# Eight weight units at other byte offsets, MoBA's score scale from a root of its own, and the first conv tap on ScalarE

## The chip, the cores and the metric

The kernel runs on one core of one Trainium2 chip. The metric is the device time of one execution, in microseconds, as the median of several executions. The engines are named as in the profile: PE is TensorE's matmul, PEld its weight load, DVE is VectorE, ACT is ScalarE, POOL is GpSimd, SP issues the DMAs.

## The reference

Two layers of a decoder trunk on x (256 tokens x 1024), all in float32. Each layer is a mixer and a feed-forward part (FFN):

```python
for l in range(DEPTH):                                   # 2
    sh1, sc1, g1, sh2, sc2, g2 = split(silu(c) @ w_mod[l] + b_mod[l], 6)
    h = rms_norm(x, mix_norm_g[l]) * (1 + sc1) + sh1
    x = x + g1 * token_mixer(h, ...)
    h = rms_norm(x, ffn_norm_g[l]) * (1 + sc2) + sh2
    x = x + g2 * channel_mixer(h, ...)

def token_mixer(h, ...):
    q_lat, kv_lat, k_rope, qkv_b, conv_in, gates = split(h @ w_in)
    o_a = MLA attention from q_lat, kv_lat, k_rope       # 8 heads
    q_b, k_b = rope(rms_norm(q, g)), rope(rms_norm(k, g))   # MoBA, 8 heads of 64
    o_b = softmax(causal(q_b @ k_b.T * 64 ** -0.5)) @ v  # one block of 256 tokens
    u = glu_a * sigmoid(glu_g)                           # 512 channels
    u = sum(w[t] * shifted(u, t) for t in range(31)) + b # causal depthwise conv
    o_c = silu(layer_norm(u)) @ w_conv_pw2 + b_conv_pw2
    return (sig(g0) * o_a @ w_mla_o + sig(g1) * o_b @ w_moba_o + sig(g2) * o_c) @ w_out

def channel_mixer(h, ...):
    a, b = split(causal_dwconv3(h @ w_up) + bias)        # 2 x 2816
    return (silu(a) * b) @ w_down
```

## The kernel before

**Weight units.** Nearly all of the matmul work goes through units. A unit is 128 x 1024 floats of weights (512 KB; some have 672 or 768 columns). SP loads it into a `raw` tile, `split` (L203) makes two fp32r tiles of it, `whi` on ACT (L210, a rounded copy) and `wlo` on DVE (L212, raw minus whi), and PE multiplies in three passes: high by high (L287), high by low of the activations (L288), low by high (L290). A unit of 1024 columns is eight 128 x 128 stationary tiles, so 24 matmuls of 256 columns. `take` (L252) hands out units in the order of `all_units` (L238) and keeps three ahead.

**Where a unit lies.** Each whi or wlo tile begins at a multiple of 512 bytes in a partition and has 128 spare columns; the unit stands in it from column `LEAD` = 16, which is 64 bytes, so every stationary tile begins at 64 bytes modulo 512. The activations that stream past (`hh`, `hl`, `oah`, `mhl` and so on) begin at 0 modulo 512.

**Order.** Each layer runs its mixer by a list of named steps, `STEPS` (L70): QKV are the MoBA projections, MS and MP the sums and the preparation for MLA, BS (`moba_rstd`, L935) and BP (`moba_prep`) the same for MoBA, MA and BA the attentions, C and G the gates, O the output projections of both attentions, V the conv taps, LN, LS, LB its layer norm, R and M the modulation of later stages, OC and PR the ends. Then come norm_stats and the FFN, in which `FFN` (L138) sets up and down units in turn: up 0, up 1, up 2, down 0, up 3 and so on, two units for each of the 22 ups, one for each down. The tile framework then schedules the instructions engine by engine, by priority in the order of the code and by its own estimate of when operands are ready; each engine runs its list strictly in order.

**MoBA's roots.** `rstd_of` (L493, L494) makes (sum * scale + eps) on DVE and raises it to -0.5 on POOL. `moba_rstd` squares q and k on ACT, sums 16 groups of 64 on DVE (L939), takes one root of 16 columns on POOL, and then DVE multiplies the 8 columns of q by 64 ** -0.5 (L942) to get `scb`, the scale of the scores. That L942 waits for POOL, and DVE's later work stands behind it.

**Conv taps.** `conv` (L1049) adds up 31 taps for each of 4 channel groups, all on DVE: tap 0 is a TENSOR_SCALAR that also adds the bias (L1054), the other 30 are L1057.

Of the kernel before, what the change touches and what calls it, by code (L numbers as in the profile page):

```python
# [10 lines left out]
F32R = mybir.dt.float32r  # L11
# [3 lines left out]
ALU = mybir.AluOpType  # L15
AX = mybir.AxisListType

P = 128
# [35 lines left out]

LINE = 512
LEAD = 16
TAILP = 2
FLEAD = 1
ROWS = [(0, 0), (0, 1), (1, 0), (1, 1)] + RPARTS
# [9 lines left out]

STEPS = [(  # L70
# [77 lines left out]
def trunk_kernel(ctx, tc, xT, crow, ccol, pos, invf, modb_d, cols_d, grow_d, wmh, wmr, wm, win1, wqkv,  # L148
# [11 lines left out]
    def nm(s):  # L160
        uid[0] += 1
        return f"{s}_{uid[0]}"
# [23 lines left out]
    def small(n, tag="sm", bufs=12):  # L186
        return wk.tile([P, n], F32, tag=tag, name=nm(tag), bufs=bufs)
# [12 lines left out]
    turn = [0]  # L200
    hold = [None]

    def split(raw):  # L203
        n = raw.shape[1]
        turn[0] += 1
        th, nh = hi_tags[turn[0] % len(hi_tags)]
        tl, nl = lo_tags[turn[0] % len(lo_tags)]
        hi, lo = (wk.tile([P, 1024 + 128], F32R, tag=t, name=nm(m), bufs=b, align_bytes=LINE)[:, LEAD:LEAD + n]
                  for t, m, b in ((th, "whi", nh), (tl, "wlo", nl)))
        ac.activation(hi, raw, AF.Copy)  # L210
        with tc.issue_after(hold[0]) if hold[0] else ExitStack():
            ve.tensor_tensor(lo, raw, hi.bitcast(F32), op=ALU.subtract)  # L212
        return hi, lo

    def chop(src, n, c, size=1024):

        m = max(1, size // c)
        return [(src[:, k0 * c:min(n, k0 + m) * c], range(k0, min(n, k0 + m))) for k0 in range(0, n, m)]

    def token_units(l, t):  # L220

        if t[0] == "KL":
            return [(win1[l, t[1], :, 0:672], [0])]
        if t[0] == "QKV":
            return [chop(wqkv[l, t[1], t[2] // 2], 4, 512)[t[2] % 2]]
        if t[0] in ("UQ", "UK"):
            return chop(wuq[l], 3, 768) if t[0] == "UQ" else chop(wukv[l], 2, 1024)
        if t[0] in ("C", "G"):
            return [chop((wgc if t[0] == "C" else wgab)[l, t[1]], KD, S)[t[2]]]
        if t[0] == "O":  # L230
            return chop(woab[l, t[1]], 1, 1024)
        if t[0] == "OC" and t[1] % 2 == 0:
            return chop(woc[l, t[1] // 2], 1, 1024)
        if t[0] == "PR" and t[1] % 2 == 0:
            return chop(wout[l, t[1] // 2], 2, 1024)
        return []

    def all_units():  # L238
        for l in range(L):
            for k in range(KD):  # L240
                if l == 0:
                    yield win1[l, k, :, 0:672], [0]
                yield win1[l, k, :, 672:1696], [0]
            for t in CFG["order"][l]:
                yield from token_units(l, t)
            for up, j in FFN:
                yield from chop(wup[l, j], KD, S) if up else chop(wdn[l, j], 1, 1024)

    ahead = [AHEAD0]
    coming, ready = list(all_units())[::-1], []  # L250
# [1 line left out]
    def take(n=1):  # L252

        while coming and len(ready) < n + ahead[0]:
            src, ks = coming.pop()
            ready.append((split(wload(src)), src.shape[1] // len(ks), ks))
        res = []
        for _ in range(n):
            (hi, lo), c, ks = ready.pop(0)
            res.append([(k, (hi[:, i * c:(i + 1) * c], lo[:, i * c:(i + 1) * c])) for i, k in enumerate(ks)])  # L260
        return res
# [226 lines left out]

    rst, rests = [None], []

    def rstd_of(ssum, n, scale):
        r = small(n, "rs", 8)
        rst[0] = ve.tensor_scalar(r, ssum, scale, EPS, op0=ALU.mult, op1=ALU.add)  # L493
        gp.tensor_tensor(r, r, mhalf[:, :n], op=ALU.pow)  # L494
        return r

# [198 lines left out]
    def layer(l):  # L695
# [239 lines left out]
        def moba_rstd(b):  # L935
            sq = mq()
            ac.activation(sq, qks[b], AF.Square)
            ss = small(16, "ss", 2)
            ve.tensor_reduce(ss, sq.rearrange("p (g d) -> p g d", d=64), axis=AX.X, op=ALU.add)  # L939
            rr = rstd_of(ss, 16, 1.0 / 64.0)  # L940
            sc = small(8, "scb", 4)
            ve.tensor_scalar(sc, rr[:, 0:8], 64 ** -0.5, None, op0=ALU.mult)  # L942
            scb.append(sc)
            rrb.append(rr)

        def moba_prep(b):
            if b == 0:
                pair = wk.tile([P, 2, 4, S], F32, tag="qkT", name=nm("qkTb"), bufs=2, align_bytes=LINE)
                qTb.append(pair[:, 0])
                kTb.append(pair[:, 1])  # L950
            rr = rrb[b]
            ra = qks[b]
            rb = mq()
            for t, i in ((rb, 1), (ra, 0)):
                for qk in range(2):
                    ve.tensor_tensor(t[:, qk * 512:(qk + 1) * 512].rearrange("p (h d) -> p h d", h=H),
                                     qks[b][:, qk * 512:(qk + 1) * 512].rearrange("p (h d) -> p h d", h=H),
                                     tb[:, i, b, qk, :].unsqueeze(1).to_broadcast([P, H, 64]), op=ALU.mult)
            av = ra.rearrange("p (g d) -> p g d", d=64)
            bv = rb.rearrange("p (g d) -> p g d", d=64)  # L960
            rope(av[..., 0:32], av[..., 32:64], av, bv, 32)
            kview = ra[:, 512:1024].rearrange("p (h d) -> p h d", h=H)
            ve.tensor_tensor(kview, kview, rr[:, 8:16].unsqueeze(2).to_broadcast([P, H, 64]), op=ALU.mult)
            for i, dst in ((0, qTb[0]), (1, kTb[0])):
                pt = psa()
                for c in range(4):
                    te.transpose(pt[:, c * P:(c + 1) * P], ra[:, i * 512 + c * P:i * 512 + (c + 1) * P], ident)
                ac.activation(dst[:, :, b * P:(b + 1) * P], pt.rearrange("p (c t) -> p c t", c=4), AF.Copy)
# [79 lines left out]
        def conv(j, t0, t1):  # L1048
            if not cacc:  # L1049
                cacc.append(wk.tile([P, 4, S], F32, tag="lh2", name=nm("cacc"), bufs=1))  # L1050
            aj = cacc[0][:, j, :]
            for t in range(t0, t1):
                if t == 0:
                    ve.tensor_scalar(aj, upad[:, j, 0:S], cw[:, j * 31:j * 31 + 1], cv(l, "cdw_b")[:, j:j + 1],  # L1054
                                     op0=ALU.mult, op1=ALU.add)
                else:
                    ve.scalar_tensor_tensor(aj, upad[:, j, t:t + S], cw[:, j * 31 + t:j * 31 + t + 1], aj,  # L1057
                                            op0=ALU.mult, op1=ALU.add)
# [301 lines left out]
```

## Time and profile before

| what | value |
|---|---|
| runs of the kernel | 928.8, 935.16, 941.89 us; median 935.16 |
| the profiled execution's own time | 937.53 us |
| its span in the profile | 935.3 us |
| PE busy | 905.6 us (97%) |
| DVE busy | 791.7 us (85%) |
| ACT busy | 554.7 us (59%) |
| POOL busy | 43.3 us (5%) |
| DMA read | 199.33 MB, 214 GB/s over the span |

Matmuls overlap each other in the pipeline, so PE can be called busy throughout a stretch and still deliver its matmuls at different spacings. For a stretch in which PE never idles, read the distance between the starts of equal instructions.

### The profile page before, as it was taken

The page shows a single profiled execution, that of the slowest core. Times are in us where ns is not written, and L with a number is a line of the kernel's source. Part 1 is how long each engine was busy: PE and PEld are TensorE (multiplying, and loading weights), DVE is VectorE, ACT ScalarE, POOL GpSimd, SP SyncE. Part 2 cuts the span into 40 slices and gives each one's busy share as a digit, 9 for nine tenths or more (in the row PEclk, how much of TensorE's full clock was granted, in tenths as well). Part 3 has the DMA queues.
Part 4 walks back from the last instruction along what each step waited for, and adds up shares of the span by engine and source line. Part 5 has one row for each costly group of instructions (what it writes and reads, how often), then busy time and mean ns, then how long its engine had stood idle before and what let it go on. Part 6 is the DMA issues. An engine that isn't in the chain of part 4 may idle for free.

```text
span 935.3 us, 18669 instructions
## 1 busy us (share of the span) xinstructions
PE 905.6 (97%) x7327; PEld 852.5 (91%) x7327; DVE 791.7 (85%) x1530; ACT 554.7 (59%) x980; POOL 43.3 (5%) x32
## 2 busy tenths in 40 slices
PE   6999989998999999999999999999999999999998
PEld 5988878988997999999979987889999799999998
DVE  6989899999987999997774999999787788777774
ACT  4677588644655655565543675895475565555551
POOL 0011500000000000000000042000000000000000
PEclk8999999999999999999999999999999999999999
DMA  8955524698868888876544565548657666655541
GB/s 308 384 194 199 181 93 165 195 320 299 301 232 287 283 266 295 298 229 193 184 151 129 184 232 182 195 129 278 223 181 264 208 226 207 189 187 189 183 134 46
DMA packets 57975, 201.59 MB, mean 216 GB/s; under 512 B 6944, under 2 KB 8480, under 8 KB 57888
## 3 DMA queue, kind: packets, MB, share of 16 engines
q1 hardware_dynamic: 57888, 200.41, 64.4%
q8 instruction: 57, 0.93, 0.4%
q14 instruction: 30, 0.25, 0.1%
HBM read 199.33 MB, written 1.05 MB: 214 GB/s over the span
## 4 chain that ended last, share of the span: by engine, by line
PE 80%; DVE 9%; DMA 5%; ACT 2%; POOL 2%; issue 2%; SPq 0%; POOLq 0%; DVEq 0%; ACTq 0%
PE psb L287 16%; PE psb L288 16%; PE psb L290 15%; PE psa L290 8%; PE psa L287 8%; PE psa L288 7%; DVE wlo L212 2%; DMA raw<-in_wmr 2%; PE psa L385 2%; POOL rs L494 2%; DVE cacc L1057 1%; PE psa L664 1%; PE psa L281 1%; PE psa L652 1%; PE psa L282 1%
## 5 line engine op out<-in xcount | busy, mean ns | idle before, releaser
L210 ACT ACTIVATE whi<-raw 128x1024 fp32r<-128x1024 f32 (+2 forms) x286 | 295.7, 1041 | 225.3 <-PE psb L288 108.4
L212 DVE TENSOR_TENSOR wlo<-raw,whi 128x1024 fp32r<-128x1024 f32 (+2 forms) x286 | 340.7, 1196 | 81.3 <-ACT whi L210 70.3
L287 PE MATMUL psb<-hh,whi 128*128 128x256 f32 x1088 | 266.3, 284 | 1.3 <-ACT thc L778 1.3
L288 PE MATMUL psb<-hl,whi 128*128 128x256 f32 x1088 | 263.1, 281 | 0.0
L287 PEld LDWEIGHTS psb<-hh,whi 128*128 128x128 f32 x1088 | 205.8, 190 | 8.7 <-issue 4.5
L288 PEld LDWEIGHTS psb<-hl,whi 128*128 128x128 f32 x1088 | 205.2, 189 | 1.4 <-DVE hl L561 1.1
L290 PE MATMUL psb<-hh,wlo 128*128 128x256 f32 x1088 | 151.2, 281 | 0.0
L290 PEld LDWEIGHTS psb<-hh,wlo 128*128 128x128 f32 x1088 | 137.4, 189 | 0.8 <-issue 0.8
L1057 DVE SCALAR_TENSOR_TENSOR cacc<-upad,cw,cacc 128x256 f32<-128x256 f32 x240 | 104.8, 480 | 0.1
L287 PE MATMUL psa<-mhl,whi 128*128 128x256 f32 x400 | 96.1, 281 | 0.0
L288 PE MATMUL psa<-mhl,whi 128*128 128x256 f32 x400 | 96.0, 281 | 0.0
L1236 DVE SCALAR_TENSOR_TENSOR e<-psb,fw,e 128x255 f32<-128x255 f32 (+1 forms) x176 | 83.9, 478 | 13.0 <-ACT e L1234 11.9
L287 PEld LDWEIGHTS psa<-mhl,whi 128*128 128x128 f32 x400 | 75.4, 189 | 0.0
L288 PEld LDWEIGHTS psa<-mhl,whi 128*128 128x128 f32 x400 | 75.4, 189 | 0.0
L494 POOL TENSOR_TENSOR rs<-rs,mhalf 128x16 f32<-128x16 f32 (+3 forms) x22 | 41.8, 1907 | 693.8 <-DVE rs L493 693.0
L1234 ACT ACTIVATE e<-psb,fb,fw 128x256 f32<-128x256 f32 x88 | 48.6, 552 | 28.3 <-DVE e L1236 14.2
L290 PE MATMUL psa<-mhl,wlo 128*128 128x256 f32 x400 | 55.0, 280 | 0.0
L368 DVE SCALAR_TENSOR_TENSOR raw<-raw,crow 128x1024 f32<-128x1024 f32 x40 | 48.9, 1222 | 4.6 <-DMA raw<-in_wmr 4.5
L290 PEld LDWEIGHTS psa<-mhl,wlo 128*128 128x128 f32 x400 | 50.5, 189 | 0.0
L287 PE MATMUL psb<-whi,hh 128*128 128x416 f32 (+1 forms) x96 | 31.6, 353 | 3.9 <-ACT hh L807 3.9
L1244 ACT ACTIVATE mhl<-e 128x256 fp32r<-128x256 f32 x44 | 18.3, 416 | 22.6 <-DVE e L1242 21.7
L288 PE MATMUL psb<-whi,hl 128*128 128x416 f32 (+1 forms) x96 | 30.7, 351 | 0.2 <-DVE hl L808 0.2
(272 smaller groups left out, 1475.3 us busy)
## 6 DMA issues: line engine op xcount, KB each, us to landing
raw<-in_wup SPq DMA_DIRECT2D x88, 512.0 KB, 4.6
raw<-in_wmr SPq DMA_DIRECT2D x52, 512.0 KB, 5.1
raw<-in_wdn SPq DMA_DIRECT2D x44, 512.0 KB, 4.3
raw<-in_wm SPq DMA_DIRECT2D x40, 512.0 KB, 4.3
raw<-in_wgab SPq DMA_DIRECT2D x32, 512.0 KB, 5.2
raw<-in_wqkv SPq DMA_DIRECT2D x24, 512.0 KB, 5.0
raw<-in_win SPq DMA_DIRECT2D x16, 512.0 KB, 4.3
raw<-in_wgc SPq DMA_DIRECT2D x16, 512.0 KB, 4.1
```

Source lines behind the costliest of these rows:

```text
L210: ac.activation(hi, raw, AF.Copy)
L212: ve.tensor_tensor(lo, raw, hi.bitcast(F32), op=ALU.subtract)
L287: te.matmul(o, p1[0], p1[1], start=start, stop=False)
L288: te.matmul(o, p2[0], p2[1], start=False, stop=False)
L290: te.matmul(o, p3[0], p3[1], start=False, stop=stop)
L368: ve.scalar_tensor_tensor(raw, raw, scale, row, op0=ALU.mult, op1=ALU.mult, accum_out=acc)
L385: te.matmul(acc[32 * c:32 * c + 32, 0:S], cact[:, k:k + 1].to_broadcast([P, 32]), raw[:, c * S:(c + 1) * S], start=(k == 0), stop=(k == KD ...
L494: gp.tensor_tensor(r, r, mhalf[:, :n], op=ALU.pow)
L1057: ve.scalar_tensor_tensor(aj, upad[:, j, t:t + S], cw[:, j * 31 + t:j * 31 + t + 1], aj, op0=ALU.mult, op1=ALU.add)
L1234: ac.activation(t, src, AF.Identity, scale=fw[:, 2, c:c + 1], bias=fb[:, c:c + 1])
L1236: ve.scalar_tensor_tensor(t[:, d:S], src[:, 0:S - d], fw[:, 2 - d, c:c + 1], t[:, d:S], op0=ALU.mult, op1=ALU.add)
L1244: ac.activation(mh, th, AF.Copy)
```

## The change

It has four parts. (1) Eight units get another offset, in four pairs that follow each other on PE: the first of a pair at 0, the second at 40 columns (160 bytes). The pairs are O6 and the first half of G7 in layer 0, the first half of G6 and O4 in layer 1, and the two halves of the FFN's up 2 in both layers. (2) `moba_rstd` takes two roots of 8 columns on POOL, first that of k, then that of q with the factor 64 folded into scale and eps, so that L942 goes. (3) In layer 0, BS0 and BS1 stand right behind MP0 and MP1. (4) Tap 0 of the conv is an activation on ACT.

```diff
+LEADS = {(0, "O", 6): 0, (0, "G", 7, 0): 40, (1, "G", 6, 0): 0, (1, "O", 4): 40}
+PAIRS = (2,)
...
-    "QKV13 QKV21 MP0 MP1 m0 QKV22 v0 MA00 MA01 MA10 MA02 BS0 MA03 MA04 C00 MA11 BS1 BP0 BP1 QKV23 C01 MA12 "
+    "QKV13 QKV21 MP0 BS0 MP1 BS1 m0 QKV22 v0 MA00 MA01 MA10 MA02 MA03 MA04 C00 MA11 BP0 BP1 QKV23 C01 MA12 "
...
-    def split(raw):
+    def split(raw, lead):
...
-        hi, lo = (wk.tile([P, 1024 + 128], F32R, tag=t, name=nm(m), bufs=b, align_bytes=LINE)[:, LEAD:LEAD + n]
+        hi, lo = (wk.tile([P, 1024 + 128], F32R, tag=t, name=nm(m), bufs=b, align_bytes=LINE)[:, lead:lead + n]
...
             for t in CFG["order"][l]:
-                yield from token_units(l, t)
+                yield from ((*u, LEADS.get((l, *t), LEAD)) for u in token_units(l, t))
             for up, j in FFN:
-                yield from chop(wup[l, j], KD, S) if up else chop(wdn[l, j], 1, 1024)
+                for i, u in enumerate(chop(wup[l, j], KD, S) if up else chop(wdn[l, j], 1, 1024)):
+                    yield *u, (0, 40)[i] if up and j in PAIRS else LEAD
...
-    def rstd_of(ssum, n, scale):
-        r = small(n, "rs", 8)
-        rst[0] = ve.tensor_scalar(r, ssum, scale, EPS, op0=ALU.mult, op1=ALU.add)
+    def rstd_of(ssum, n, scale, eps=EPS):
+        r = small(n, "rs", 12)
+        rst[0] = ve.tensor_scalar(r, ssum, scale, eps, op0=ALU.mult, op1=ALU.add)
...
-            rr = rstd_of(ss, 16, 1.0 / 64.0)
-            sc = small(8, "scb", 4)
-            ve.tensor_scalar(sc, rr[:, 0:8], 64 ** -0.5, None, op0=ALU.mult)
-            scb.append(sc)
-            rrb.append(rr)
+            rrb.append(rstd_of(ss[:, 8:16], 8, 1.0 / 64.0))
+
+            scb.append(rstd_of(ss[:, 0:8], 8, 1.0, 64.0 * EPS))
...
                 if t == 0:
-                    ve.tensor_scalar(aj, upad[:, j, 0:S], cw[:, j * 31:j * 31 + 1], cv(l, "cdw_b")[:, j:j + 1],
-                                     op0=ALU.mult, op1=ALU.add)
+                    ac.activation(aj, upad[:, j, 0:S], AF.Identity, scale=cw[:, j * 31:j * 31 + 1],
+                                  bias=cv(l, "cdw_b")[:, j:j + 1])
```

The pairs move nothing in any engine's list; the other parts do. The changed kernel's lines from 203 on stand two to four lower, so that L958 there is L956 here.

On DVE in layer 0, where MoBA's sums meet the first MLA attention (mq are MoBA's q and k, tb its rotary table, mx the row maxima and nb the biases of the MLA scores, cacc the conv's sum). Before:

```order
L493 TENSOR_SCALAR rs_1457<-ss_1455 128x16
L956 TENSOR_TENSOR mq_1463<-mq_923,tb_753 128x512
L1057 SCALAR_TENSOR_TENSOR cacc_1258<-upad_773,cw_762,cacc_1258 128x256
L612 TENSOR_REDUCE mx_1277<-psa_1264 128x2
L612 TENSOR_REDUCE mx_1277<-psa_1265 128x2
L942 TENSOR_SCALAR scb_1460<-rs_1457 128x8
L956 TENSOR_TENSOR mq_1463<-mq_923,tb_753 128x512
L615 TENSOR_SCALAR nb_1281<-mx_1277 128x8
```

And in the changed kernel, in the same place:

```order
L958 TENSOR_TENSOR mq_1465<-mq_923,tb_753 128x512
L1059 SCALAR_TENSOR_TENSOR cacc_1278<-upad_773,cw_762,cacc_1278 128x256
L613 TENSOR_REDUCE mx_1297<-psa_1283 128x4
L616 TENSOR_REDUCE mx_1297<-psa_1284 128x2
L616 TENSOR_REDUCE mx_1297<-psa_1285 128x2
L1059 SCALAR_TENSOR_TENSOR cacc_1278<-upad_773,cw_762,cacc_1278 128x256
L619 TENSOR_SCALAR nb_1301<-mx_1297 128x8
```

The sums of both row blocks now stand ahead of the maxima, and between the maxima and nb there is no instruction that reads a root from POOL.

On ACT in layer 0, behind the latents (klt are the KV latents, whi the units of the query and key-value projections). Before:

```order
L862 ACTIVATE klt_772<-psb_864,col_133 128x256
L210 ACTIVATE whi_889<-raw_887 128x768
L210 ACTIVATE whi_907<-raw_905 128x768
L210 ACTIVATE whi_929<-raw_927 128x1024
L896 ACTIVATE mq_923<-psa_810 128x512
```

And in the changed kernel:

```order
L866 ACTIVATE klt_772<-psb_864,col_133 128x256
L213 ACTIVATE whi_889<-raw_887 128x768
L1056 ACTIVATE cacc_1278<-upad_773,col_133,cw_762 128x256 x3
L213 ACTIVATE whi_907<-raw_905 128x768
L1056 ACTIVATE cacc_1278<-upad_773,col_133,cw_762 128x256
L213 ACTIVATE whi_929<-raw_927 128x1024
L900 ACTIVATE mq_923<-psa_810 128x512
```

The four taps stand between whi copies that are wanted by PE.

## Rows read from the trace of the kernel before

**Rows 1.** The page: busy time by engine, and the chain that ended last.

```profile
PE 905.6 (97%) x7327; PEld 852.5 (91%) x7327; DVE 791.7 (85%) x1530; ACT 554.7 (59%) x980; POOL 43.3 (5%) x32
...
PE 80%; DVE 9%; DMA 5%; ACT 2%; POOL 2%; issue 2%; SPq 0%; POOLq 0%; DVEq 0%; ACTq 0%
```

**Rows 2.** Timeline of PE, layer 1, conv input units: start, us, what, count.

```profile
490.38 1.07 PE L290 MATMUL psa<-hh,wlo 128*128 128x256 f32 x8
...
506.70 1.07 PE L290 MATMUL psa<-hh,wlo 128*128 128x256 f32 x8
```

**Rows 3.** Chain in order of time, FFN of layer 0: start, us, what.

```profile
309.05 0.94 PE psa L290 x8
...
467.35 0.94 PE psa L290 x8
```

**Rows 4.** Timeline of PE, FFN of layer 0, second half of up 2.

```profile
304.80 0.28 PE L288 MATMUL psb<-hl,whi 128*128 128x256 f32 x1
305.55 0.44 PE L393 MATMUL psa<-ident,e 128*128 128x128 f32 x2 [0.47 <-ACT e L390]
305.75 0.36 PE L287 MATMUL psb<-hh,whi 128*128 128x256 f32 x1
305.95 0.28 PE L288 MATMUL psb<-hl,whi 128*128 128x256 f32 x1
306.06 1.10 PE L290 MATMUL psb<-hh,wlo 128*128 128x256 f32 x8
```

**Rows 5.** Timeline of PE, layer 1, around the conv norm's broadcast (L523).

```profile
675.78 0.50 PE L290 MATMUL psb<-hh,wlo 128*128 128x256 f32 x3
676.12 0.60 PE L523 MATMUL psb<-ident,rs 128*128 128x128 f32 x4
678.45 1.11 PE L290 MATMUL psb<-hh,wlo 128*128 128x256 f32 x8
```

**Rows 6.** Stretches: PE, PEld, DVE, ACT, POOL busy (count), PEclk, DMA share, GB/s.

```profile
190.00:235.00 45.00, 40.40 (x351) 38.83 (x351) 41.51 (x83) 19.47 (x26) 0.77 (x1) 1.00 0.88 305
...
306.00:470.00 164.00, 164.00 (x1394) 164.00 (x1394) 143.75 (x253) 93.79 (x139) 0.00 (x0) 1.00 0.76 248
...
760.00:925.00 165.00, 165.00 (x1401) 164.83 (x1400) 124.75 (x200) 90.89 (x136) 0.00 (x0) 1.00 0.54 170
```

**Rows 7.** Timeline of DVE, layer 0, MoBA's sums and the first MLA attention.

```profile
105.84 1.22 DVE L212 TENSOR_TENSOR wlo<-raw,whi 128x1024 fp32r<-128x1024 f32 x1
109.86 0.17 DVE L942 TENSOR_SCALAR scb<-rs 128x8 f32<-128x8 f32 x1 [2.79 <-POOL rs L494]
...
116.40 0.17 DVE L942 TENSOR_SCALAR scb<-rs 128x8 f32<-128x8 f32 x1 [1.20 <-POOL rs L494]
...
117.08 0.16 DVE L615 TENSOR_SCALAR nb<-mx 128x8 f32<-128x8 f32 x1
```

**Rows 8.** Waits of PE, 55 to 290 us: who, for whom, us, times, longest.

```profile
PE psb L523 <- POOL rs L494: 3.0, 2, 2.4
PE psa L652 <- ACT p L643: 2.5, 2, 2.2
PE psb L287 <- DVE b L1117: 1.9, 1, 1.9
```

**Rows 9.** Waits in layer 1, 525 to 740 us: one row of DVE's, one of PE's.

```profile
DVE scb L942 <- POOL rs L494: 1.7, 2, 1.2
```

```profile
PE psa L597 <- ACT p L631: 1.0, 1, 1.0
```

**Rows 10.** POOL's roots by width: busy us, mean ns, idle before.

```profile
L494 POOL TENSOR_TENSOR rs<-rs,mhalf 128x16 f32<-128x16 f32 x8 | 25.6, 3196 | 55.6 <-DVE rs L493 55.5
L494 POOL TENSOR_TENSOR rs<-rs,mhalf 128x8 f32<-128x8 f32 x4 | 7.6, 1900 | 0.7 <-PE psa L288 0.7
```

**Rows 11.** The tap on DVE, by line: duration min/median/max in ns.

```profile
L1054 DVE TENSOR_SCALAR cacc<-upad,cw,col x8: 400/408/411, 63.0 to 598.2; 128x256 f32<-128x256 f32 x8
```

**Rows 12.** ACT: an activation of the tap's form, then the timeline around the taps' place.

```profile
L1093 ACT ACTIVATE e<-e,col 128x256 f32<-128x256 f32 x8 | 4.7, 587 | 0.0
```

```profile
70.46 0.85 ACT L210 ACTIVATE whi<-raw 128x768 fp32r<-128x768 f32 x1 [1.09 <-PE psa L288]
73.20 1.06 ACT L210 ACTIVATE whi<-raw 128x1024 fp32r<-128x1024 f32 x1 [1.90 <-PE psa L288]
```

More of the change, by code (lines that the diff above doesn't have):

```diff
@@ L241, in all_units @@
                 if l == 0:
-                    yield win1[l, k, :, 0:672], [0]
-                yield win1[l, k, :, 672:1696], [0]
+                    yield win1[l, k, :, 0:672], [0], LEAD
+                yield win1[l, k, :, 672:1696], [0], LEAD
             for t in CFG["order"][l]:
-                yield from token_units(l, t)
+                yield from ((*u, LEADS.get((l, *t), LEAD)) for u in token_units(l, t))
             for up, j in FFN:
-                yield from chop(wup[l, j], KD, S) if up else chop(wdn[l, j], 1, 1024)
+                for i, u in enumerate(chop(wup[l, j], KD, S) if up else chop(wdn[l, j], 1, 1024)):
+                    yield *u, (0, 40)[i] if up and j in PAIRS else LEAD
     ahead = [AHEAD0]
@@ L254, in take @@
         while coming and len(ready) < n + ahead[0]:
-            src, ks = coming.pop()
-            ready.append((split(wload(src)), src.shape[1] // len(ks), ks))
+            src, ks, lead = coming.pop()
+            ready.append((split(wload(src), lead), src.shape[1] // len(ks), ks))
         res = []
@@ L962, in moba_prep @@
             kview = ra[:, 512:1024].rearrange("p (h d) -> p h d", h=H)
-            ve.tensor_tensor(kview, kview, rr[:, 8:16].unsqueeze(2).to_broadcast([P, H, 64]), op=ALU.mult)
+            ve.tensor_tensor(kview, kview, rr.unsqueeze(2).to_broadcast([P, H, 64]), op=ALU.mult)
             for i, dst in ((0, qTb[0]), (1, kTb[0])):
```

## The prediction

> **What bounds the kernel now.** I read the busy times first, then the chain, then the spacing of PE's matmuls, then the waits. PE is busy 97% of the span and holds 80% of the chain [rows 1], so time is won either where PE idles or where its matmuls follow each other faster. PE's idle time is small: in layer 0 the three long waits are for POOL's root, for ACT's p and for DVE's b, 3.0 + 2.5 + 1.9 = 7.4 us [rows 8]; in layer 1 one of 1.0 us counts here [rows 9].
>
> The spacing is the larger thing. A unit of 24 matmuls ends with eight L290. In layer 1's conv input the first and the last of seven such rows lie 506.70 - 490.38 = 16.32 us apart, six units, so 2.72 us a unit or 113.3 ns a matmul [rows 2]. In layer 0's FFN the first and the last of 57 lie 467.35 - 309.05 = 158.30 us apart, 56 units, so 2.827 us a unit or 117.8 ns [rows 3]. Engine, tile shape, column count and granted clock (1.00, [rows 6]) are the same, and PE never idles there. So the same work runs at one of two spacings, 0.107 us a unit apart, and neither changes for dozens of units. The rows show where it changes. In layer 0's FFN it is fast until PE has two transposes of another kind after a short idle, and slow from there: eight L290 take 1.10 us, against 1.07 in a fast unit [rows 2, 4]. In layer 1 it is fast ahead of the broadcast L523 and slow from the unit behind it (1.11 us) [rows 5]. The spacing is thus a state that PE keeps while units of one layout follow each other, and that something of another kind can reset. Both FFNs spend it slow: 164.00 us for 1394 matmuls and 165.00 for 1401 are 117.6 and 117.8 ns each [rows 6].
>
> **The change part by part.**
>
> *The pairs.* What differs in the eight units is where the stationary tiles begin, 0 and 160 bytes instead of 64, while the streamed ones stay at 0. It costs nothing itself: split issues the same instructions, and the spacing inside eight units is worth 8 x 0.107 = 0.9 us if all of them ran at the other level. What counts is the state behind a pair, when the units are at 64 bytes again. Each pair stands at the head of a long slow stretch: behind L523 in both layers (that of layer 1: [rows 5]), and in the FFN the second half of up 2 is the very unit that the transposes interrupt, with ten matmuls left [rows 4]. No row shows a unit at another offset, so the effect is bounded from both sides by the two levels: nothing, or the whole of the slow stretches behind the pairs. In units: each FFN has 19 more ups of two units and 22 downs, 60 units x 0.107 = 6.4 us, twice 12.8; layer 1 from 682 us, behind O4, to 731, where the layer's mixer ends, 49 us / 2.827 = 17 units, 1.8 us; layer 0 from G7 to the next slow end at 245 us about 3 units, 0.3 us. Sum 14.9 us. PE is on the path throughout there. Would another engine stop it? In layer 0's FFN DVE is busy 143.75 of 164 us [rows 6]; with 6.2 us less that is 91%, and the DMA share goes from 0.76 to 0.79, under the 0.88 of the stretch at 190 us. So the gain would arrive. I take the upper end: the trace shows that the state is kept only as long as the layout of operands is one and the same, and that every change in kind it holds (transposes, broadcasts) is a place where the state may turn; a change of offset is the nearest thing to these, at places where only the fast side is left to turn to.
>
> A rule speaks against it. The Trainium skill, TensorE: Matmul & The Clock Gate, section "Step-by-step: what each phase is for", says that PE reads the stationary operand through a port of its own and that loading the next tile takes no read bandwidth from the running matmul. By it the place of a unit would not matter and this term would be 0 instead of 14.9 us. The trace does not agree with a single spacing: 113.3 and 117.8 ns for one form [rows 2, 3]; but it doesn't show that the place is the reason.
>
> *MoBA's roots and the moved sums, layer 0.* DVE waits 2.79 and 1.20 us for POOL in front of L942 [rows 7], in a stretch where it is otherwise never idle; nb, which starts the first attention's exponentials, stands behind the second. With the roots taken earlier and no L942, neither wait is left: the next reader of a root is the multiplication of k, which stands behind nb. Four roots of 8 columns cost POOL 4 x 1.90 = 7.6 us against 2 x 3.20 = 6.4 [rows 10]; POOL is idle enough to hide 1.2 us more, and they start some 2 us earlier. The 3.99 us that DVE gets back bring nb, and with it ACT's p, forward by more than PE's wait for p, so of those 2.5 us I take 2.2. DVE then has 3.99 - 2.2 = 1.8 us in hand.
>
> *The taps.* Four taps a layer leave DVE, 4 x 0.41 = 1.6 us [rows 11] of which the pipelined part is some 1.3. On ACT four cost about 4 x 0.59 = 2.3 us [rows 12]; in layer 0 they stand among whi copies in front of which ACT idles 1.09 and 1.90 us for PE [rows 12], and in layer 1 among whi copies that wait likewise. That hides them; without that cover each tap would hold up a whi by 0.59 us, 4.7 us for eight, which is the bad end. DVE's first L1057 of each group now waits for ACT; queued behind it are wlo and the latents' low parts, for which PE waits. But the taps are done some 6 us ahead of most of the conv.
>
> With 1.8 + 1.3 = 3.1 us in hand at 190 us, PE's waits for b (1.9) and for the root behind the conv's norm (2.4 of the 3.0) could shrink [rows 8]; against that the DMA share there is 0.88 at 305 GB/s [rows 6], and a wait for a load takes DVE's place. Between 0 and 3.1 I take 1.5.
>
> *Layer 1.* DVE gets 1.7 us of waits back [rows 9] and 1.3 us of taps, again ahead of nb; PE's wait there is 1.0 us [rows 9], and I take 1.1 with the smaller ones after it.
>
> Scheduling together: 2.2 + 1.5 + 1.1 = 4.8 us, between -1 (taps uncovered, 4.7 lost, roots gained) and 7.
>
> **Sum.** The profiled execution took 937.53 us, 2.4 above the median of the three runs. 937.5 - 14.9 - 4.8 = 917.8, so 918. That is 1.8% below the median of 935.16; 2%, about what a measurement of this kernel tells from no change, lies at 916.5.
>
> **The rivals.**
>
> *One kind of pair works, the other doesn't.* The FFN pairs are broken by the transposes, so that only the step from 160 to 64 bytes acts there, and it may turn the state in one layer only, since the transposes cut the unit after 14 matmuls in layer 0 and elsewhere in layer 1. Then 6.4 us are missing: 924.2. For it: the state turned at L523 and at the transposes by itself, so timing of a few ns seems to decide. Against it: both FFNs ended in the same state before.
>
> *The place of a unit doesn't matter* (the rule above). The states fall as they fall, slow as in the profile: 937.5 - 4.8 = 932.7. For it: no row shows an offset act; the 64-byte units keep whichever state they have whatever buffer they lie in. Against it: nothing but an operand's layout or timing is left to part two spacings of one form.
>
> *A slower lock.* A pair leaves PE in a third state. No row shows one; if it lay as far above the slow one as that above the fast, 0.107 us a unit, the two FFNs would lose 120 x 0.107 = 12.8 us: 937.5 + 12.8 - 4.8 = 945.5, slower than before. It decides from the first unit behind up 2, and any spacing above 117.8 - 4.8 us / (120 x 24) = about 119.5 ns in both FFNs would eat the scheduling gain. For it: slow is not shown to be the slowest. Against it: in a whole trace of resets PE only ever fell to these two.
>
> **How the numbers follow.** Forecast 0.52 (912 to 923), one FFN only 0.20 (921 to 928), place of no matter 0.20 (929 to 937), slower lock 0.08. The runs before spread over 13.1 us, about two FFNs' worth, so states may turn from run to run; that widens each case by some 3 us. The range 912 to 934 leaves out 0.02 below, and above it the slow lock and about half of the third case, 0.18. Faster by over 2%, below 916.5: four tenths of the forecast's own chance, where scheduling gives over 6 us or the median's scale applies, 0.21, plus 0.02 from the others, 0.23. Slower by over 2%, above 953.9, needs twice the third state's price: 0.02. Within: 0.75.
>
> **What would show it.** In the changed profile, eight L290 in both FFNs at 1.07 us and units 2.72 us apart say the pairs act; 1.10 and 2.83 say they don't; more is the slower lock. In layer 1 behind O4 the same. DVE should show no wait for POOL at 105 to 120 us, PE's wait for p in layer 0 should be gone, and ACT should show the four taps with no longer wait of PE for a whi near 65 to 75 us. I would be wrong above all if the state is set by chance at each reset, and next if DMA waits swallow what DVE gains at 190 to 233 us.

## The result, and the profile of the changed kernel

| kernel | runs | median, us | lowest to highest, us |
|---|---|---|---|
| before | 20 | 931.64 | 925.26 to 942.73 |
| changed | 20 | 938.12 | 928.72 to 951.18 |

The ratio is 1.0053, with a 95% interval of 1.0028 to 1.0078: half a per cent slower, where 918 us and a gain were forecast. 938.12 lies outside the range as well. Ratios, here and below, leave out runs over 1.5% above the fastest of the same kernel, so they are not quite the quotient of the medians, which are of all runs.

The profiled execution of the changed kernel took 930.16 us, 8 under the median, and its span is 7.6 us shorter than that of the profile before. So the first thing to see is that this one trace doesn't stand for the median. The page's busy times and its chain:

```profile
PE 897.6 (97%) x7327; PEld 842.2 (91%) x7327; DVE 786.3 (85%) x1522; ACT 557.7 (60%) x988; POOL 52.9 (6%) x36
...
PE 73%; DVE 13%; DMA 5%; ACT 4%; issue 3%; POOL 1%; SPq 0%; POOLq 0%; DVEq 0%; ACTq 0%
```

PE is busy 8.0 us less than in [rows 1], and DVE has gone from 9% to 13% of the chain. Both have a place. The stretches of the changed kernel (columns as in [rows 6]):

```profile
306.00:462.00 156.00, 156.00 (x1379) 156.00 (x1378) 140.69 (x248) 91.46 (x136) 0.00 (x0) 1.00 0.78 257
...
560.00:570.00 10.00, 6.58 (x50) 4.93 (x49) 10.00 (x24) 4.84 (x8) 9.48 (x4) 0.93 0.63 193
570.00:580.00 10.00, 7.70 (x35) 5.52 (x36) 6.30 (x11) 3.17 (x5) 1.83 (x1) 0.55 0.21 72
...
760.00:915.00 155.00, 155.00 (x1369) 155.00 (x1369) 120.04 (x193) 90.00 (x134) 0.00 (x0) 1.00 0.58 179
```

Both FFNs run at the fast spacing: 156.00 / 1379 = 113.1 ns and 155.00 / 1369 = 113.2 ns, against 117.6 and 117.8 in [rows 6]. That is the spacing that the forecast counted on; whether the pairs made it is for the experiments. PE's timeline in the FFN of layer 0 shows it at the pair, beside [rows 4]:

```profile
300.11 1.12 PE L294 MATMUL psb<-hh,wlo 128*128 128x256 f32 x8
...
303.28 0.44 PE L397 MATMUL psa<-ident,e 128*128 128x128 f32 x2 [0.37 <-ACT e L394]
...
303.79 1.13 PE L294 MATMUL psb<-hh,wlo 128*128 128x256 f32 x8
...
306.60 1.07 PE L294 MATMUL psa<-mhl,wlo 128*128 128x256 f32 x8
```

The unit at 0 bytes (1.12 us for its last eight matmuls) and the unit at 160 (1.13) are slower than either level of before (1.07 and 1.10); the unit behind them is fast. (L291, L292 and L294 are before's L287, L288 and L290.)

What took back half of it stands between 560 and 580 us, in layer 1, where the first MLA attention (MA) starts. In the profile before the same two slices read

```profile
560.00:570.00 10.00, 10.00 (x52) 8.37 (x51) 8.30 (x15) 5.34 (x7) 5.87 (x2) 1.00 0.58 175
570.00:580.00 10.00, 10.00 (x82) 7.57 (x80) 10.00 (x23) 5.00 (x9) 0.00 (x0) 1.00 0.55 162
```

PE was busy throughout at a clock of 1.00. Now it idles from 566.6 to 572.3 us, and from 568.7 to 578.9 the granted clock is 0.50, the lower of its two levels (1.2 GHz instead of 2.4). The waits there, first DVE's (515 to 590 us), then PE's (540 to 600 us):

```profile
DVE ma L1011 <- POOL rs L498: 2.5, 1, 2.5
DVE ma L1023 <- POOL rs L498: 1.5, 1, 1.5
```

```profile
PE psa L599 <- ACT qkT L1041: 5.7, 1, 5.7
```

L1011 and L1023 are in MLA's preparation (`mla_prep`, the step MP): they multiply its queries (ma) and keys (kv) by their roots. L1041 copies the transposed queries and keys to qkT, and L599 begins the scores. Neither of DVE's two waits stands in the profile before, and PE did not wait at this place there; its one wait of that window, 1.0 us [rows 9], is another, for p. The chain in order of time joins them:

```profile
545.08 2.05 POOL rs L498
...
547.94 4.25 POOL rs L498
...
563.57 1.12 DVE wlo L215
564.73 5.96 DMA raw<-in_wgc
570.71 1.06 ACT whi L213
571.77 0.49 ACT qkT L1041
572.30 1.22 PE psa L599 x4
```

DVE waits for POOL's root, so its wlo copies come late; a wlo frees a raw buffer, so the load of wgc starts only at 564.73 and lands at 570.71; ACT's whi copy waits for it, and the qkT copies that PE wants are queued behind that whi on ACT. From the end of layer 1's conv input (498 us) to 660 us the changed kernel goes from 6.9 us ahead to 0.9 behind: 7.8 us lost. It is still 7.0 ahead at 561.67 and 1.2 ahead when the scores start, so 5.8 go in PE's wait; 3.1 go while the clock is low, and 1.0 comes back, about what the wait for p [rows 9] took before.

### The profile page after: what moved, and what is told of

Its sections match the earlier page's. It is cut to its first block, busy times and chain, and to the rows that moved or that the text cites. A ratio compares the mean times of both kernels' runs of the same rounds, so it can differ in the third digit from the quotient of the medians.

```text
span 927.7 us, 18675 instructions
## 1 busy us (share of the span) xinstructions
PE 897.6 (97%) x7327; PEld 842.2 (91%) x7327; DVE 786.3 (85%) x1522; ACT 557.7 (60%) x988; POOL 52.9 (6%) x36
## 4 chain that ended last, share of the span: by engine, by line
PE 73%; DVE 13%; DMA 5%; ACT 4%; issue 3%; POOL 1%; SPq 0%; POOLq 0%; DVEq 0%; ACTq 0%
PE psb L291 14%; PE psb L292 14%; PE psb L294 14%; PE psa L291 6%; PE psa L292 6%; PE psa L294 6%; DVE wlo L215 5%; PE psa L389 2%; DVE cacc L1059 2%; DMA raw<-in_wmr 2%; ACT whi L213 2%; DVE raw L736 1%; DMA raw<-in_wup 1%; PE psa L601 1%; POOL rs L498 1%
## 5 line engine op out<-in xcount | busy, mean ns | idle before, releaser
L291 PE MATMUL psb<-hh,whi 128*128 128x256 f32 x1088 | 261.8, 282 | 1.6 <-ACT thc L782 1.5
L292 PE MATMUL psb<-hl,whi 128*128 128x256 f32 x1088 | 258.7, 279 | 0.0
L291 PEld LDWEIGHTS psb<-hh,whi 128*128 128x128 f32 x1088 | 204.9, 189 | 8.7 <-issue 4.9
L292 PEld LDWEIGHTS psb<-hl,whi 128*128 128x128 f32 x1088 | 204.8, 188 | 1.4 <-DVE hl L565 0.8
L294 PE MATMUL psb<-hh,wlo 128*128 128x256 f32 x1088 | 148.2, 278 | 0.0
L294 PEld LDWEIGHTS psb<-hh,wlo 128*128 128x128 f32 x1088 | 134.9, 188 | 0.8 <-issue 0.8
L291 PE MATMUL psa<-mhl,whi 128*128 128x256 f32 x400 | 93.3, 276 | 0.0
L292 PE MATMUL psa<-mhl,whi 128*128 128x256 f32 x400 | 93.1, 277 | 0.0
L498 POOL TENSOR_TENSOR rs<-rs,mhalf 128x8 f32<-128x8 f32 (+3 forms) x26 | 51.4, 1990 | 683.2 <-DVE rs L497 683.1
L291 PEld LDWEIGHTS psa<-mhl,whi 128*128 128x128 f32 x400 | 74.9, 188 | 0.1
L292 PEld LDWEIGHTS psa<-mhl,whi 128*128 128x128 f32 x400 | 74.9, 188 | 0.0
L294 PE MATMUL psa<-mhl,wlo 128*128 128x256 f32 x400 | 53.5, 276 | 0.0
L294 PEld LDWEIGHTS psa<-mhl,wlo 128*128 128x128 f32 x400 | 49.1, 188 | 0.0
L291 PE MATMUL psb<-whi,hh 128*128 128x416 f32 (+1 forms) x96 | 32.0, 358 | 4.4 <-ACT hh L811 4.4
L389 PE MATMUL psa<-raw,cact 128*32 128x256 f32 x320 | 31.5, 434 | 0.0
```

What stands on the lines that cost most here:

```text
L291: te.matmul(o, p1[0], p1[1], start=start, stop=False)
L292: te.matmul(o, p2[0], p2[1], start=False, stop=False)
L294: te.matmul(o, p3[0], p3[1], start=False, stop=stop)
L389: te.matmul(acc[32 * c:32 * c + 32, 0:S], cact[:, k:k + 1].to_broadcast([P, 32]), raw[:, c * S:(c + 1) * S], start=(k == 0), stop=(k == KD ...
```

## The experiments

All times below are medians, with the ratio to the kernel before on the same chip and its 95% interval in brackets; e7_places, e10_places2 and e11_again were run once each, for their profiles.

**Parts alone and parts taken out.** Four kernels, each a subset of the diff. e1_pairs is the kernel before with

```
+LEADS = {(0, "O", 6): 0, (0, "G", 7, 0): 40, (1, "G", 6, 0): 0, (1, "O", 4): 40}
+PAIRS = (2,)
```

and what hands a unit's place to split.

> The kernel before with the eight units at 0 and 160 bytes and nothing else of the change. Theory P (the pairs turn PE to the fast spacing in nearly every execution, and what the changed kernel lost, it lost in layer 1 by the other edits): both FFNs fast, eight matmuls of the last pass in 1.07 us, PE gap ahead of L601's first scores at most 1.1 us as before, and 10 us under the kernel before, some 921. Theory Q (the spacing is drawn anew at each disturbance of each execution whatever the place of a unit; the profiled execution was a lucky one): no difference beyond 2 us, and the FFNs fast or slow.

Measured: 931.21, ratio 0.9989 [0.9954, 1.0024]. That is theory Q's time. Whether Q's reason holds, one profile can't say. The profiled execution (936.14 us) has layer 0's FFN fast and layer 1's slow, and behind O4 of layer 1 it is fast. In layer 1's FFN PE's timeline reads:

```profile
753.08 1.07 PE L294 MATMUL psb<-hh,wlo 128*128 128x256 f32 x8
...
755.90 1.12 PE L294 MATMUL psb<-hh,wlo 128*128 128x256 f32 x8
...
758.55 0.44 PE L397 MATMUL psa<-ident,e 128*128 128x128 f32 x2
...
759.18 1.12 PE L294 MATMUL psb<-hh,wlo 128*128 128x256 f32 x8
...
762.03 1.11 PE L294 MATMUL psa<-mhl,wlo 128*128 128x256 f32 x8
```

The same unit at 0, the same unit at 160 cut by the transposes, and slow behind it (1.11), where the changed kernel was fast. Taken together, six profiled executions had the pairs at up 2: layer 0's FFN came out fast in six of six, layer 1's in two of six. The pair at G60 and O4 of layer 1, which nothing interrupts, left PE fast in all six. Seven other profiles (before, e2_nopairs, and e6_pair3 to e10_places2 below, ahead of their own moved units) have up 2 at 64 bytes, with the same transposes in it: there layer 0's FFN came out fast in two of seven and layer 1's in five of seven. On these counts the cut pair helped in layer 0 and not in layer 1; over both layers 8 of 12 with it stand against 7 of 14 without, which fits a time that hardly moves. In the mixers and in layer 0 the counts speak for the place, against Q.

e2_nopairs: `LEADS = {}` and `PAIRS = ()` in the changed kernel.

> The changed kernel with all units at 64 bytes again; roots, moved sums and taps stay. Theory P: the FFNs slow, 13 us over the changed kernel, some 948 to 951, with the 5.7 us wait of PE in layer 1 still there. Theory Q: the changed kernel's 938 within 2 us; the wait in layer 1 is there all the same.

Measured: 937.79, ratio 1.0069 [1.0033, 1.0105]. Theory P's 948 is wrong: without pairs layer 0's FFN was fast all the same in the profiled execution (946.87 us, the longest of its runs) and layer 1's slow. So the FFNs of a kernel without pairs aren't always slow, as the one profile before made me think. DVE's two waits and a gap of 5.3 us on PE were there.

e3_notaps: the tap back to `ve.tensor_scalar` (L1056).

> The changed kernel with the first conv taps on DVE again. If the taps on ACT make the wait of 5.7 us in layer 1 (and the clock's fall to 0.55 behind it): the wait is under 1.5 us and the time 6 to 8 us under the changed kernel, 930 to 932. If the roots or the moved sums make it: the wait stays, 938 within 2 us.

Measured: 927.18, ratio 0.9956 [0.9925, 0.9987], some 1% under the changed kernel, more than the 6 to 8 us expected. DVE's two waits are gone, and PE's is small:

```profile
PE psa L599 <- ACT qkT L1041: 0.7, 1, 0.7
```

e4_oldroots: one root of 16 columns, scb and the old steps of BS back; pairs and taps stay.

> The changed kernel with one root of 16 columns and its scaling on DVE again, and the sums at their old steps; pairs and taps stay. If the roots make the wait in layer 1: it is under 1.5 us and the time 930 to 932. If the taps make it: it stays, and the time is 938, or 2 us more as layer 0 gets its wait for p back.

Measured: 935.09, ratio 1.0043 [1.0008, 1.0078]. The waits of 2.5 and 1.5 us stay (at L1013 and L1025 here), PE's gap is 4.0 us. So the taps make the wait, with either kind of root. In layer 0 PE's wait for p, 0.2 us in the changed kernel, is back at 2.4 us with the old roots.

**How the taps make it.** At their place they cost PE nothing: layer 1's last tap starts at 505.1 us, and at 561.67 PE is as far ahead of the profile before as at 498. In the build they change DVE's order some 35 us later. The changed kernel's order on DVE there, and that of e5_taps0, which has the taps on ACT in layer 0 alone:

```
changed kernel
804 L497 TENSOR_SCALAR rs_6853<-ss_6849 128x16
805 L1004 TENSOR_REDUCE kss_6858<-ma_6856 128x8
806 L1011 TENSOR_TENSOR ma_6715<-ma_6715,rs_6853 128x8x64
807 L497 TENSOR_SCALAR rs_6860<-kss_6858 128x8
808 L996 TENSOR_REDUCE ss_6926<-ma_6924 128x8

e5_taps0
805 L497 TENSOR_SCALAR rs_6853<-ss_6849 128x16
...
807 L1004 TENSOR_REDUCE kss_6858<-ma_6856 128x8
808 L996 TENSOR_REDUCE ss_6926<-ma_6924 128x8
...
813 L1011 TENSOR_TENSOR ma_6715<-ma_6715,rs_6853 128x8x64
```

L497 hands a sum to POOL for its root, and L1011 wants the root. In e5_taps0 seven rows lie between L497 and L1011, a wlo of 1.22 us among them; in the changed kernel one does. e5_taps0's edit, with the arguments cut to `...`:

```
+if l == 0:
     ac.activation(aj, upad[:, j, 0:S], AF.Identity, scale=..., bias=...)
+else:
+    ve.tensor_scalar(aj, upad[:, j, 0:S], ..., op0=ALU.mult, op1=ALU.add)
```

> The changed kernel with the first taps on ACT in layer 0 alone; layer 1 has them on DVE. In the build DVE's order in layer 1 is then that of the kernel before again: the multiplication of a head's queries by their root (L1011) stands behind the next batch's sum (L996) and not ahead of it. If that order is what loses the time: no wait of DVE for POOL of 2.5 and 1.5 us in front of L1011 and L1023 (layer 1), PE's gap ahead of L599 under 1.1 us, clock 1.00 there, and a median like that of e3_notaps, 927 within 3 us. If instead the work of the taps on ACT costs the time: the layer 0 half of it is left, some 932.

Measured: 926.47, ratio 0.9934 [0.9896, 0.9972]. The two waits are gone; what is left of DVE's waits from 515 to 590 us is

```profile
DVE wlo L215 <- ACT whi L213: 0.6, 1, 0.6
DVE mx L613 <- PE psa L604: 0.3, 1, 0.3
```

and PE's gap is 0.4 us. The time is that of e3_notaps: four taps on ACT in layer 0 cost and bring nothing that can be measured, and the whole loss comes with layer 1's taps. That it is the order they bring, and not their work on ACT, is argued from PE's lead of 7.0 us at 561.67 and from the two waits; no run has layer 1's taps on ACT with DVE's old order.

**Pairs that nothing interrupts.** e6_pair3 is e3_notaps with `PAIRS = (3,)`; e8_pairs3_alone is the kernel before with the pairs and `PAIRS = (3,)`. PE runs the two units of up 3 one right after the other.

> The changed kernel without taps on ACT, and the pair of the FFN at up 3 instead of up 2: two units that PE runs one right after the other, with no transposes in between. If a pair that is not interrupted always leaves PE at the fast spacing (as the eight pairs of the mixers seen so far did) and an interrupted one leaves it by chance: in both layers 120 ns in the two units of up 3 and 113.3 ns in every unit behind; the median 2 to 4 us under e3_notaps, some 924, and the spread of the runs smaller. If the outcome is chance anyway: one of the FFNs slow now and then, 927.

> The kernel before with the pairs alone, the FFN's at up 3. If an uninterrupted pair always works: both FFNs fast, 3 us under e1_pairs, some 928, against 933.7 of the kernel before. If the outcome is chance: e1_pairs' 931.

Measured: 923.99 (922.65 to 926.61), ratio 0.9896 [0.9845, 0.9947], and 926.58 (923.67 to 931.41), ratio 0.9920 [0.9890, 0.9950]. Both expectations held. Both FFNs are fast in both profiles, and the runs lie within 4 and 8 us, those of the kernel before on the same chip within 17.5. PE's timeline of e6_pair3 in layer 0's FFN:

```profile
301.90 1.10 PE L294 MATMUL psb<-hh,wlo 128*128 128x256 f32 x8
...
304.73 1.11 PE L294 MATMUL psa<-mhl,wlo 128*128 128x256 f32 x8
...
307.59 1.12 PE L294 MATMUL psb<-hh,wlo 128*128 128x256 f32 x8
...
310.47 1.11 PE L294 MATMUL psb<-hh,wlo 128*128 128x256 f32 x8
...
313.23 1.07 PE L294 MATMUL psb<-hh,wlo 128*128 128x256 f32 x8
```

Slow behind the transposes, the pair, and fast. In all profiles together a whole unit at 0 followed by a whole unit at 160 and then by units at 64 came 17 times, and PE was fast behind all 17. e6_pair3 is 1.0% faster than the kernel before.

**What a place does.** In e7_places, otherwise as e3_notaps, the FFN's units lie at a series of places (the lists are cut at `...`):

```
+PLACES = {(0, j): (v, v) for j, v in ((4, 0), (5, 8), (6, 24), (7, 32), (8, 40), (9, 48), ...)}
+PLACES |= {(1, 4): (0, 16), (1, 6): (40, 16), (1, 8): (0, 40), (1, 10): (40, 0), ...}
-                    yield *u, (0, 40)[i] if up and j in PAIRS else LEAD
+                    yield *u, PLACES.get((l, j), (LEAD, LEAD))[i] if up else LEAD
```

> No pairs in the FFNs but a series of places, everything else as in e3_notaps. In layer 0 both units of ups 4 to 20 lie at one place each: 0, 32, 96, 128, 160, 192, 224, 256, 288, 320, 352, 384, 416, 448, 480, 16 and 80 bytes; in layer 1 the two units of an up lie at 0 and 64, 160 and 64, 0 and 160, 160 and 0, 64 and 0, 64 and 160, 0 and 160, 160 and 160, 0 and 0. The units between are at 64. If the place of a stationary tile sets the spacing: every unit at 0 has 120 ns, every one at 160 the pattern 118 to 125, and other places have values of their own; behind 160 the units at 64 run at 113.3, and the single unit at 160 does it without the one at 0. If the spacing were only a state that a change of place may turn: 113.3 or 117.8 at every place.

Starts of the first matmuls around two ups of e7_places (L295 is its first pass), at 0 bytes and at 192 bytes, each with its 48 matmuls:

```profile
312.24 0.28 PE L295 MATMUL psb<-hh,whi 128*128 128x256 f32 x1
...
318.00 0.28 PE L295 MATMUL psa<-mhl,whi 128*128 128x256 f32 x1
```

```profile
354.59 0.28 PE L295 MATMUL psb<-hh,whi 128*128 128x256 f32 x1
...
360.03 0.28 PE L295 MATMUL psa<-mhl,whi 128*128 128x256 f32 x1
```

(318.00 - 312.24) / 48 = 120.0 ns, and (360.03 - 354.59) / 48 = 113.3. In the same way, for all places of layer 0 (slow is 117.8 ns, fast is 113.3, reached after one unit at 114.0 behind 128):

| place, bytes | ns a matmul | the unit at 64 behind it |
|---|---|---|
| 0, 256 | 120.0 | slow |
| 16 | 118.4 | slow |
| 32, 288 | 118.3 | slow |
| 80 | 118.8 | slow |
| 96, 352 | 117.3 | fast |
| 128, 384 | 118.5 | fast |
| 160, 416 | 119.8 | fast |
| 192, 448 | 113.3 | fast |
| 224, 480 | 116.6 | fast |
| 320 | 117.8 | slow |

In this series the place sets the spacing, places 256 bytes apart are alike, and 320 (64 + 256) keeps the slow spacing that it finds. In layer 1 every unit at 0 left PE slow and every one at 160 fast, with and without the other of the pair. From this alone one would drop the unit at 0, or put everything at 192.

e9_single drops it, `LEADS = {(0, "G", 7, 0): 40, (1, "O", 4): 40}` and `(LEAD, 40)[i]` in e6_pair3:

> e6_pair3 with the four units at 0 put back to 64 bytes: what is left of each pair is its unit at 160. If the unit at 160 alone turns PE to the fast spacing: the units behind it at 113.3 ns in both FFNs and behind O4 of layer 1, and e6_pair3's time less some 0.5 us (four units, two in each layer, at 113 to 118 instead of 120 ns), 923.5 within 2 us. If both are needed: the FFNs keep the spacing that the transposes leave, 927 to 931.

Measured: 924.68 (923.35 to 928.03), ratio 0.9925 [0.9898, 0.9952]. The time is as expected for 160 alone, but the reason holds only in part. Both FFNs were fast already ahead of the unit at 160 in the profiled execution, so its trace proves nothing for them; the runs lie within 4.7 us, less than the 6 us of one slow FFN, which speaks for 160 alone being enough there. In layer 1, PE was slow behind the broadcast (L527), and the unit at 160 did not turn it: 118 ns on average in the units of the 56 us behind. From a slow stretch at 64 bytes a single unit at 160 thus left PE fast twice (e7_places, layer 1) and slow once. With the unit at 0 ahead it never failed; why, and whether the FFN needs both, isn't shown.

e10_places2 puts a unit at 0 ahead of each of 17 places in layer 0.

> A second series of places. In layer 0 the first unit of ups 4 to 20 lies at 0, which has left PE slow every time, and the second at 192, 96, 224, 32, 128, 112, 144, 176, 208, 240, 80, 48, 160, 320, 448, 352, 480 bytes; in layer 1 the ups lie at 192 and 192, 160 and 192, 0 and 192, 96 and 64, 0 and 64, 224 and 64, 0 and 64, 144 and 64, 176 and 64. If 192 is like 64, a place that keeps the spacing it finds: 117.8 behind 0 and 113.3 behind 160. If 192 is a place of its own that is always fast: 113.3 behind both, and the units at 64 behind it fast. 96 and 160 should leave PE fast, 0, 32 and 80 slow, and places 256 bytes apart should be alike.

The unit at 192 behind the one at 0 (120 ns) is fast at once, (318.92 - 316.20) / 24 = 113.3 ns:

```profile
316.20 0.28 PE L295 MATMUL psb<-hh,whi 128*128 128x256 f32 x1
...
318.92 0.28 PE L295 MATMUL psa<-mhl,whi 128*128 128x256 f32 x1
```

It was fast behind 0, behind 160 and behind 64, in all seven cases of the two kernels (192 and 448); the units at 64 ahead of it were already fast, so entry from slow units at 64 was never tried. Other places show that what PE did before counts as well: 128 bytes behind a unit at 0 left PE slow, where it left it fast in e7_places behind fast units; 176 left it fast behind 0 and slow behind fast units at 64; and 96 ran at 117.4 ns behind 0, but at 120.1 behind fast units at 64. This is the evidence on which e12_all192 stood: `LEAD = 48`, no pairs, no taps on ACT.

> The changed kernel without taps on ACT and without pairs, with every unit at 192 bytes instead of 64 (LEAD = 48). If 192 bytes is a place that is fast whatever PE did before: every one of the some 5,600 matmuls of 256 columns with a stationary tile of a unit at 113.3 ns once its unit is under way, none at 117.8 for long, in both FFNs and in the mixers; the time that of e6_pair3 less the 3 us that it still lost, 921 within 2 us, with a spread of the runs under 5 us. If 192 was fast only for the states that it was entered from: slow stretches as in the kernel before, 927 to 934.

Measured: 938.99 (926.70 to 945.14), ratio 1.0016 [0.9971, 1.0060]. The theory of a place that is always fast falls: in the profiled execution, of 5,487 distances under 130 ns from one matmul of a unit to the next, 49 are near 113 ns and nearly all others near 118, with units 2.83 us apart:

```profile
306.42 1.10 PE L294 MATMUL psa<-mhl,wlo 128*128 128x256 f32 x8
...
309.25 1.10 PE L294 MATMUL psb<-hh,wlo 128*128 128x256 f32 x8
...
312.08 1.10 PE L294 MATMUL psb<-hh,wlo 128*128 128x256 f32 x8
```

192 is like 64 a place with two spacings that keeps the one it falls into; behind a unit at 0 it fell into the fast one each time.

**The changed kernel once more**, unaltered, for a second profile.

> The changed kernel as it is, once more, for a second execution's profile. If the outcome of the interrupted pairs is chance, one of the FFNs can be slow here, and the time then lies 6 us above 930, 936; with both fast 930. DVE's waits of 2.5 and 1.5 us for POOL, PE's wait of some 5 us ahead of L599 and the clock's fall behind it stand in the order of the program and should be there again.

Its execution took 931.01 us, with layer 0's FFN fast and layer 1's slow (936 was expected for that), and PE's gap of 5.5 us ahead of L599 with DVE's waits ahead of it, to the tenth as before:

```profile
DVE ma L1011 <- POOL rs L498: 2.5, 1, 2.5
...
DVE ma L1023 <- POOL rs L498: 1.5, 1, 1.5
```

The clock behind it is 0.83 and 0.82 in 560 to 570 and 570 to 580 us, where the first profile has 0.93 and 0.55.

## Why the prediction was wrong

Two terms failed: the 14.9 us for the pairs, of which about 1 came, and the 1.1 us for the taps and layer 1, in whose place some 9 us were lost. By the runs, each kernel being the one before it plus a part: the pairs (e1_pairs) take the ratio from 1 to 0.9989, the roots and moved sums (e3_notaps) to 0.9956, the taps (the changed kernel) to 1.0053. In us that is -1, -3 and +9, each uncertain by 3 to 4, where the forecast had -14.9 and, for the rest together, -4.8. It also counted from the profiled execution's 937.5 us, 6 above the median of 20 runs.

**The pairs, -14.9 us: half right.** The likeliest case said that an offset turns the state at places where only the fast side is left. The mechanism is real. The term failed in two ways. First, the base: I took the slow stretches of one profile for those of the kernel. With up 2 at 64 bytes an FFN was slow in seven of fourteen cases, and the runs of before spread over 17 us, about as much as the forecast's own two FFNs and layer 1's mixer (14.6 us); the gain against a median is about half of the term. Measured with pairs that always work (e8_pairs3_alone), it is 0.8%, 7.5 us. That the state falls by chance is what the prediction named as its first way to be wrong. Second, the place: the pair at up 2 is cut by the transposes, and layer 1's FFN then came out fast in two of six, no oftener than without a pair (five of seven). That was the rival "one kind of pair works, the other doesn't", which should have been the forecast: the argument for it, that the transposes cut the unit elsewhere in layer 1, stood in my own text. With the pairs cut, e1_pairs gains 1 us, by its interval between 4.3 gained and 2.2 lost. That layer 1's FFN was fast as well in the first profile of the changed kernel was luck.

**The place doesn't matter** (rival, 0.20): wrong. The Trainium skill, TensorE: Matmul & The Clock Gate, section "Step-by-step: what each phase is for", says that the load of the next stationary tile takes no read bandwidth from the running matmul. The runs disagree with what the prediction drew from it, that the place then doesn't matter: with nothing but the stationary tile's place changed, the distance from one matmul to the next goes from 113.3 to 120.0 ns (e7_places). Whether the load takes bandwidth from the matmul they don't show.

**A slower lock** (rival, 0.08): units at 0 and 160 do run at 120 ns, a third level, but only while they last. (In that rival's sum the 119.5 ns are 117.8 plus 1.7; the minus sign is a slip.)

**MoBA's roots, layer 0, -2.2 us: right.** PE's wait of 2.2 us for p [rows 8] is gone (0.2 is left, and with the old roots it is back), and so are DVE's waits for POOL at 98 to 125 us [rows 7]. POOL's 8-column roots cost more than the 1.90 us taken from [rows 10]:

```profile
L498 POOL TENSOR_TENSOR rs<-rs,mhalf 128x8 f32<-128x8 f32 x12 | 30.5, 2561 | 13.3 <-DVE rs L497 13.3
```

but that stays off PE's path in e3_notaps. Two comparisons on one chip differ by the roots and steps alone: from e1_pairs to e3_notaps the median falls by 4.0 us, from e8_pairs3_alone to e6_pair3 by 2.6. Both fit the forecast, though in each the intervals of the ratios overlap.

**The waits at 190 to 233 us, -1.5: half.** In the changed kernel's profile PE's wait for b is 2.1 us, where [rows 8] has 1.9; the 2.4 us for the root behind the conv's norm are gone, and 0.4 ahead of the norm's sums (L519) stand in their place. The profiles scatter here: that second gap lay between 0.3 and 2.4 us in those of the experiments.

**The taps and layer 1, -1.1: the step that failed.** I priced a tap by its duration (0.59 us, which it has: eight taps of 587 to 601 ns) and by what waits for it on ACT, and let DVE's freed 1.3 us arrive at nb. I didn't ask whether the build, which chooses the order, would leave DVE's order in layer 1 as it was. The listing of the changed order showed L1011 moved up to one row behind L497; I read it in layer 0 only. The two waits for POOL stand ahead of wlo copies, and 7.8 us were lost in the profiled execution instead of 1.1 gained. PE's wait of 1.0 us for p, from which the term was taken, did go; the wait at the scores stands in its place. e5_taps0 and e3_notaps show that layer 1's taps do it; that they do it by the order is argued above.

**The sum again, between the two profiles:** the slow spacing's excess over 113.3 ns, summed over the distances under 130 ns between matmuls of units, is 18.2 us before and 4.2 after, -14.0; the start of layer 1's attention costs +7.8; the rest, -1.4, is left for layer 0 and the small waits. Together -7.6, the difference of the spans. So in these two executions the pairs' term seems to have come whole; in e11_again, the same kernel, the excess is 10.4 us.

**What stays open.** The profiled executions of the changed kernel (930.2 and 931.0) lie low in its own spread, and layer 1's FFN explains 6 us of it and not all. The taps cost some 9 us by the runs and 7.8 in the profile. The median of the granted clocks of the changed kernel's runs is 0.982 (0.985 and 0.989 in the two profiles), that of e2_nopairs and e4_oldroots, which share the wait, 0.985, and that of the other kernels 0.986 to 0.990; so part of the loss may be the clock behind the wait, which fell differently in the two profiles. Why a place sets the spacing, and what decides the state behind a disturbance, the runs don't show.

## What to carry to other kernels

Before a term is taken from one profile, ask whether the state that it prices is the same in every execution: a spread of the runs as large as the term says that it isn't, and a fix that makes the state certain was here worth about half of it, and a narrower spread. An edit that moves an instruction from one engine to another is not priced by its own duration where a scheduler sets the order: read the new order on every engine that gets or loses work, above all between a request to a slow engine and the reader of its answer. A device that resets a state must itself not be interrupted: moved by one up, the same pairs went from no measurable gain to 0.8%.

## What the hardware showed that was not expected

- The spacing of matmuls of one shape (256 columns, clock 1.00) depends on where the stationary tile begins, alike for places 256 bytes apart, with the streamed tile at a multiple of 512: 120.0 ns at 0, 116.6 to 119.8 at the other places of e7_places, and 113.3 or 117.8 at 64 and 192 bytes, where it keeps the value that it falls into for hundreds of matmuls. What ran before counts too: 96 bytes gave 117.4 ns in one case and 120.1 in another (e10_places2).
- A unit at 0 leaves PE at the slow spacing every time; from there a whole unit at 160 left it fast 17 times of 17, and one at 192 runs fast itself. A unit at 160 alone, from slow units at 64, left PE slow once in three cases, behind a broadcast.
- At 160 bytes the spacing repeats with a period of six matmuls, 118, 121, 117, 125, 116, 123 ns.
- POOL's root of 8 columns took 1.90 us in one profile [rows 10] and 2.56 on average in the other; why isn't shown.
